# Rotary tables loaded in the opening, memory keys/values through the weights' staging, roundings behind late transfers moved on ScalarE

## The chip, the cores and the metric

One NeuronCore of a Trainium2 chip runs the whole program. Its engines are TensorE (PE in the profile, with PEld for the loading of stationary operands), VectorE (DVE), ScalarE (ACT), GpSimd (POOL) and SyncE (SP), which here only issues DMAs. Time is in device microseconds (us), from runs of the same program on the chip; lower is better. Each engine takes its instructions in the order in which they stand in its program; engines wait for each other through semaphores.

## The reference

An encoder trunk of two layers on 1024 tokens of width 1024, with 256 memory tokens, all in float32. The first layer mixes tokens by windowed attention (16 heads that share 4 key/value heads, rotary positions, a sink per head), the second by a gated linear recurrence (HGRN2, 8 heads, both directions). In both, four further heads attend to the memory tokens. Each layer ends with a gated feed-forward part.

```python
mem_n = rmsnorm(mem, mem_norm_g)
for layer in range(DEPTH):
    u = rmsnorm(h, norm_g[layer, 0])
    mem_kv = mem_n @ w_mem_kv[layer]
    if kind == 0:
        y = mixer_window_attn(u, mem_kv, a_w_in[slot], a_sink[slot], a_w_out[slot], pos)
    elif kind == 1:
        y = mixer_hgrn2(u, mem_kv, b_w_in[slot], lb[0, layer], lb[1, layer], b_norm_g[slot], b_w_out[slot])
    ...
    h = h + rmsnorm(y, norm_g[layer, 1])
    f = conv_ffn(rmsnorm(h, norm_g[layer, 2]), ...)
    h = h + rmsnorm(f, norm_g[layer, 3])

def rope(x, pos):
    ...
    cos = jnp.cos(ang)[None, :, None, :]
    sin = jnp.sin(ang)[None, :, None, :]
    x1, x2 = xf[..., :half], xf[..., half:]
    return jnp.concatenate([x1 * cos - x2 * sin, x2 * cos + x1 * sin], axis=-1)
```

## The kernel before

Every matrix product is made of three products of rounded parts: an operand x is held as h (x rounded to the matmul's format, a copy on ACT) and l (x minus h, a subtraction on DVE), and `mm3` (L82 to L85) adds h·h, h·l and l·h. So every weight and every activation goes through an ACT instruction and a DVE instruction before PE can use it. In the profile L78/L79 are that pair in `wunit`, L88/L89 in `split`, L415/L416 in `read`, L364/L365 in `attend`, L1281/L1282 in `scaled`.

**Weights.** `wunit` (L69) loads one unit of 512 KB through SP's queue into a staging tile `st` (pool `stg`, 4 buffers) and splits it into `wh` and `wl` (pool `ring`, 4 buffers). With `parts=2` the load and the split are made in two halves; only the first unit is.

**Order.** The program is written in one order, and a scheduler orders each engine's instructions by a simulated time with the written order as priority. `tc.issue_after(ins)` queues those instructions of a block that run on the engine of `ins` behind `ins`. Pools are stacked in SBUF; one that is opened after another's release takes its place and waits for its tiles one by one.

**The opening, `start` (L1264).** `memory_kv` (L150) makes keys and values of the memory for both layers: for each layer four units of key weights (`wmk`) and four of value weights (`wmv`), each followed by a `step()` that hands out one piece of side work: the memory's own norm (`memory_rstd`, which also loads the identity), the eight rows `xT` of the transposed input, rounded into `uh`/`ul` (`part`), and the sums of squares of the eight token blocks of x (`square`, ACT, L1293). The results are written to DRAM (`kvd`). Before its first matmul stand the scaled memory columns `mh`/`ml` (8 of them, from `memT`, `scaled`), whose four loads are issued on ACT's queue.

**The first mixer, `window` (L236).** At its head the tables `cos` and `sin` are loaded through SP's queue (L243, L244) into the pool `attn0`, then the window's mask and the sinks. For each of four groups `proj(g)` (L261) projects eight token tiles (24 matmuls each, `pj`, two PSUM banks), rotates them on DVE (L286, L287) with the tables, adds on POOL (L288, L289) and takes v out of PSUM (L291 on ACT, L292 on DVE), which frees the bank. In group 0 `rooted` (L1255) first scales each token tile's part of the tables by its norm. Each add on POOL of group 0 also sends on `second_sums` (L124): a copy of feed-forward weights from DRAM to DRAM on POOL's queue (`w2s`, 1 MB).

`attend(g)` (L313) goes over eight blocks n of 128 tokens: scores, exponentials (L338, ACT), scaling, transposes, product with v, and a copy of the result out of PSUM into `o` (L357, L358). After each second block `o` goes to DRAM (`oT`), or, in group 3, straight into chunks 6 and 7 of `ul` in SBUF (L363), where it is rounded (L364, L365). Between the blocks `cross_unit` (L191) handles the memory heads; its result leaves PSUM by a copy `xo` (L232) from the only bank `po`.

**The first mixer's output, class `Out` (L392).** `begin` (L436) reads chunks 0 to 5 of each token tile back from `oT` (`read`, L411: DMA on SP's queue, then rounding on ACT and DVE) and multiplies them (`kept`) into y0 (copy L448); `finish` adds the rest. `begin` is written after `attend(3)`, but the scheduler spreads it through that time.

**The second mixer, `hgrn` (L925).** For each of eight heads: `proj`, four calls of `direction` (two directions, two halves of the tokens), `output`. `direction` works in the tiles `E` (pool `hg0`, 5 buffers). In the even heads `cross` (L1204) puts two cross units in: with the first, `cross_head` (L184) loads that memory head's keys/values from `kvd` into a tile `kv`, which is one of the five `E` buffers (L1212), splits it into `kvh`/`kvl` (one buffer) and loads the query weights `wxq`.

Of the kernel before, what the change touches and what calls it, by code (L numbers as in the profile page):

```python
# [8 lines left out]
F32 = mybir.dt.float32  # L9
F32R = mybir.dt.float32r  # L10
# [8 lines left out]
P = 128  # L19
# [28 lines left out]
def build(tc, A, out):  # L48
# [20 lines left out]
    def wunit(src, n=1024, pl=None, eng=None, parts=1):  # L69

        tg = ("wh", "wl") if pl is None else ("xwh", "xwl")
        h = (pl or ring).tile([P, 1024], F32R, tag=tg[0], name=tg[0])
        l = (pl or ring).tile([P, 1024], F32R, tag=tg[1], name=tg[1])
        raw = stg.tile([P, 1024], F32, tag="st", name="st")[:, :n]
        for p in range(parts):
            c = slice(p * n // parts, (p + 1) * n // parts)
            nc.sync.dma_start(raw[:, c], src[:, c])
            act.copy(h[:, c], raw[:, c])  # L78
            (eng or dve).tensor_tensor(l[:, c], raw[:, c], h[:, c].bitcast(F32), op=ALU.subtract)  # L79
        return h, l  # L80
# [155 lines left out]
    def window():  # L236
# [4 lines left out]
        cos = ea.tile([P, NT, 32], F32, name="cos")  # L241
        sin = ea.tile([P, NT, 2, 32], F32, name="sin")
        nc.sync.dma_start(cos, A["cos"])  # L243
        nc.sync.dma_start(sin, A["sin"])  # L244
# [67 lines left out]

        def attend(g, qkv):  # L313
            qs, kh, kl, v = qkv
            for b in range(2):
                for nn in range(4):
# [20 lines left out]
                    for j in range(4):  # L337
                        act.activation(sm[:, j, :w], sm[:, j, :w], AF.Exp, bias=st["nm"][:, j:j + 1], scale=0.125,  # L338
                                       accum_out=st["su"][:, j:j + 1])
# [19 lines left out]
                    if nn % 2 == 1 and g == 3:  # L359
                        ts_ = slice((n - 1) * P, (n + 1) * P)  # L360
                        oh, ol = uh[:, 6:8, ts_], ul[:, 6:8, ts_]
                        for hp in range(2):
                            nc.sync.dma_start(ul[hp * 64:(hp + 1) * 64, 6:8, ts_].bitcast(F32), o[:, hp::2, :])  # L363
                        act.copy(oh, ol.bitcast(F32))  # L364
                        dve.tensor_tensor(ol, ol.bitcast(F32), oh.bitcast(F32), op=ALU.subtract)  # L365
                    elif nn % 2 == 1:
                        ts_ = slice((n - 1) * P, (n + 1) * P)
                        for hp in range(2):
                            nc.sync.dma_start(
                                oT[0][2 * g:2 * g + 2, hp * 64:(hp + 1) * 64, ts_].rearrange("a d t -> d a t"),  # L370
                                o[:, hp::2, :])
# [11 lines left out]
        ea.release()  # L383
        attend(3, cur)
        wo0.open()
        y0 = wo0.w1.tile([P, NT, 512], F32, bufs=1, name="y0")
        wo0.begin(psq, ("pj", "pj", "ptq"), [y0[:, t, :] for t in range(NT)])
# [4 lines left out]
    class Out:  # L392
# [18 lines left out]
        def read(self, ks, c0, c1, eng):  # L411
            c = (slice(None), slice(ks[0], ks[-1] + 1), slice(c0, c1))
            raw = ul[c].bitcast(F32)
            eng.dma_start(raw, oT[self.l][ks[0]:ks[-1] + 1, :, c0:c1].rearrange("k p t -> p k t"))
            act.copy(uh[c], raw)  # L415
            dve.tensor_tensor(ul[c], raw, uh[c].bitcast(F32), op=ALU.subtract)  # L416
# [19 lines left out]
        def begin(self, psb, tags, y0):  # L436
            self.psb, self.y0 = psb, y0
            self.banks += [(psb, t, tags.count(t)) for t in tags]
            eng = (nc.sync, act)[self.l]
            for i, t in enumerate(self.order):  # L440
                if i < 2:
                    with tc.high_priority(AHEAD):
                        self.read(self.groups[0], t * P, (t + 1) * P, eng)
                else:
                    self.read(self.groups[0], t * P, (t + 1) * P, eng)
                ps = self.bank()
                self.kept(ps, t, self.groups[0], True, True)
                act.copy(y0[t], ps)  # L448
            self.used = 0
# [475 lines left out]
    def hgrn():  # L925
# [278 lines left out]
        def cross(n):  # L1204
# [3 lines left out]
            for _ in range(n):  # L1208
                xh_, xb_ = units.pop(0)
                if xhead[1] != xh_:  # L1210
                    xhead[1] = xh_
                    raw = early.tile([P, 512], F32, tag="E", bufs=5, name="kv")  # L1212
# [40 lines left out]
    xss = x0.tile([P, NT], F32, name="xss")  # L1253

    def rooted(t, *tables):  # L1255
# [3 lines left out]
        for x in tables:  # L1259
            dve.tensor_scalar_mul(x, x, rs0[:, c])  # L1260
# [3 lines left out]
    def start():  # L1264
# [8 lines left out]
        pool.memset(ones, 1.0)  # L1273
        act.activation(ones[:, 0:1], ones[:, 0:1], AF.Square)
        act.dma_start(gT, A["gT"])
        first = [wunit(A["wmk"][0, 0], parts=2)]
        for k in range(0, KT, 2):
            act.dma_start(mT[:, k:k + 2], A["memT"][:, k:k + 2])

        def scaled(h, l, raw, g):  # L1280
            act.activation(h, raw, AF.Identity, scale=g)  # L1281
            dve.scalar_tensor_tensor(l, raw, g, h.bitcast(F32), op0=ALU.mult, op1=ALU.subtract)  # L1282

        for k in range(KT):
            scaled(mh[:, k], ml[:, k], mT[:, k], gT[:, 0, k:k + 1])
# [9 lines left out]
        def memory_rstd():  # L1295
# [3 lines left out]
            nc.sync.dma_start(ident, A["ident"])  # L1299
            dve.tensor_scalar(mss, mss, 1.0 / D, EPS, op0=ALU.mult, op1=ALU.add)  # L1300
# [124 lines left out]
```

## Time and profile before

| | us |
|---|---|
| runs shown, median (lowest to highest) | 2672.87 (2672.17 to 2677.5) |
| the profiled execution's own time | 2679.56 |
| its span, first to last instruction | 2677.8 |
| mean granted TensorE clock | 0.993 |

The profile is of one execution. A row of a timeline gives the start, the duration, the engine, the line, the operation, what it writes and reads, the number of instructions merged, and in brackets how long the engine was idle before it and what ended that. A row of windows gives a stretch, its length, the busy time and the number of instructions of each engine (PE, PEld, DVE, ACT, POOL), the granted clock of PE, the share of the DMA engines and GB/s. A row of waits reads: who waited, for whom, in total, times, longest. A row of the chain gives start, length and what the end waited for.

### The profile page before, as it was taken

How to read it: one execution, taken by the hardware profiler on the slowest of the kernel's cores; microseconds unless marked ns; L12 is line 12 of the kernel's file. 1: busy time of each engine (PE TensorE's matmuls, PEld its weight loads, DVE VectorE, ACT ScalarE, POOL GpSimd, SP SyncE). 2: the span in 40 equal slices, each digit the busy share in tenths (PEclk: the TensorE clock that was granted, in tenths of full speed). 3: DMA queues.
4: the chain of work that ended last, by engine and by line, in shares of the span. 5: the costliest groups of instructions: out<-in, count | busy, mean ns of one | idle time of the engine just before them, and what ended most of it. 6: DMA issues, size and time to landing. Idle time of an engine off the chain costs nothing.

```text
span 2677.8 us, 39101 instructions
## 1 busy us (share of the span) xinstructions
PE 2612.1 (98%) x14420; PEld 2192.2 (82%) x14420; DVE 1814.1 (68%) x3041; ACT 1379.2 (52%) x2501; POOL 471.8 (18%) x519
## 2 busy tenths in 40 slices
PE   8899999999999999999999999999999999999998
PEld 7788887788888887887887888888788788888887
DVE  5588786578565655478778686886757755656447
ACT  6467676545444444454455554545534444444443
POOL 0331110211111100032223142230211111110013
PEclk9899999999999999999999999999999999999999
DMA  9583123367777757574325252102436778774666
GB/s 359 203 196 71 60 75 103 96 186 184 207 194 201 204 157 241 195 242 150 99 96 163 76 128 62 48 29 90 143 119 176 193 195 210 197 203 160 225 191 235
DMA packets 195728, 425.93 MB, mean 159 GB/s; under 512 B 20048, under 2 KB 56272, under 8 KB 189904
## 3 DMA queue, kind: packets, MB, share of 16 engines
q1 hardware_dynamic: 161552, 324.59, 37.7%
q0 software_dynamic: 24544, 90.19, 16.2%
q10 hardware_dynamic: 9440, 8.66, 1.0%
q8 instruction: 113, 1.85, 0.3%
q14 instruction: 79, 0.65, 0.1%
HBM read 330.04 MB, written 116.39 MB: 167 GB/s over the span
## 4 chain that ended last, share of the span: by engine, by line
PE 77%; DVE 13%; DMA 4%; ACT 3%; issue 2%; POOL 1%; SPq 0%; ACTq 0%; DVEq 0%; POOLq 0%
PE X L521 27%; PE V L521 11%; PE pj L83 5%; PE pj L84 5%; PE pj L85 5%; PE Y L521 5%; PE pb L83 3%; PE pb L85 3%; PE pb L84 3%; DVE E L1077 1%; DVE ER L1112 1%; PE pt L351 1%; PE po L1180 1%; DVE wl L89 1%; DVE wl L79 1%
## 5 line engine op out<-in xcount | busy, mean ns | idle before, releaser
L89 DVE TENSOR_TENSOR wl<-st,wh 128x1024 fp32r<-128x1024 f32 (+1 forms) x238 | 262.6, 1110 | 326.9 <-ACT wh L88 283.3
L88 ACT CAST wh<-st 128x1024 fp32r<-128x1024 f32 (+1 forms) x238 | 222.5, 937 | 295.7 <-PE X L521 194.0
L83 PE MATMUL pj<-uh,wh 128*128 128x512 f32 x512 | 205.4, 402 | 2.2 <-DVE q L1022 1.4
L521 PE MATMUL X<-wl,wh 128*128 128x512 f32 x528 | 205.3, 391 | 0.3 <-DVE wl L89 0.3
L521 PE MATMUL X<-wh,wl 128*128 128x512 f32 x528 | 205.1, 390 | 0.0
L84 PE MATMUL pj<-ul,wh 128*128 128x512 f32 x512 | 203.1, 397 | 0.1
L83 PE MATMUL pj<-wh,uh 128*128 128x384 f32 (+1 forms) x512 | 190.6, 373 | 13.0 <-DVE v L292 9.2
L85 PE MATMUL pj<-uh,wl 128*128 128x512 f32 x512 | 202.7, 396 | 0.0
L521 PE MATMUL X<-wh 128*128 128x512 f32 x528 | 199.5, 391 | 2.2 <-ACT c L894 2.2
L85 PE MATMUL pj<-wh,ul 128*128 128x384 f32 (+1 forms) x512 | 187.5, 367 | 0.0
L84 PE MATMUL pj<-wl,uh 128*128 128x384 f32 (+1 forms) x512 | 187.3, 366 | 0.0
L79 DVE TENSOR_TENSOR wl<-st,wh 128x1024 fp32r<-128x1024 f32 (+2 forms) x94 | 118.5, 1267 | 36.4 <-ACT wh L78 35.7
L521 PE MATMUL V<-uh,wh 128*128 128x512 f32 x344 | 133.8, 389 | 0.0
L521 PE MATMUL V<-ul,wh 128*128 128x512 f32 x344 | 133.8, 389 | 0.0
L521 PE MATMUL V<-uh,wl 128*128 128x512 f32 x344 | 133.8, 389 | 0.0
L78 ACT CAST wh<-st 128x1024 fp32r<-128x1024 f32 (+2 forms) x100 | 99.8, 1006 | 45.3 <-PE pj L84 28.5
L521 PEld LDWEIGHTS X<-wh 128*128 128x128 f32 x528 | 99.5, 188 | 23.5 <-ACT c L894 2.6
L521 PEld LDWEIGHTS X<-wl,wh 128*128 128x128 f32 x528 | 99.6, 189 | 21.3 <-DVE wl L89 0.7
L83 PEld LDWEIGHTS pj<-wh,uh 128*128 128x128 f32 x512 | 97.0, 189 | 24.4 <-issue 9.4
L521 PEld LDWEIGHTS X<-wh,wl 128*128 128x128 f32 x528 | 99.4, 188 | 20.8
L83 PEld LDWEIGHTS pj<-uh,wh 128*128 128x128 f32 x512 | 97.4, 190 | 22.1 <-DVE q L1022 2.2
L85 PEld LDWEIGHTS pj<-uh,wl 128*128 128x128 f32 x512 | 97.2, 190 | 19.7
(388 smaller groups left out, 7163.0 us busy)
## 6 DMA issues: line engine op xcount, KB each, us to landing
st<-hid SPq DMA_DIRECT2D x154, 256.0 KB, 3.0
st<-in_ffw_dram SPq DMA_DIRECT2D x108, 256.0 KB, 3.3
w2s<-in_ffw_dram POOLq DMA_DIRECT2D x24, 1024.0 KB, 7.8
st<-in_ffw_dram SPq DMA_DIRECT2D x46, 512.0 KB, 4.2
hid<-tt SPq DMA_DIRECT2D x88, 256.0 KB, 4.8
st<-w2s SPq DMA_DIRECT2D x88, 256.0 KB, 3.3
sx<-in_ffw_dram SPq DMA_DIRECT2D x84, 256.0 KB, 4.0
sy<-in_ffw_dram SPq DMA_DIRECT2D x42, 512.0 KB, 6.5
```

Of the source, the lines that this page charges most:

```text
L78: act.copy(h[:, c], raw[:, c])
L79: (eng or dve).tensor_tensor(l[:, c], raw[:, c], h[:, c].bitcast(F32), op=ALU.subtract)
L83: pe.matmul(o, ah, bh, start=first, stop=False)
L84: pe.matmul(o, ah, bl, start=False, stop=False)
L85: pe.matmul(o, al, bh, start=False, stop=last)
L88: act.copy(h, src)
L89: dve.tensor_tensor(l, src, h.bitcast(F32), op=ALU.subtract)
L351: pe.transpose(tp[:, j, :], sm[:, j, c * P:(c + 1) * P], ident)
L521: pe.matmul(o, x, y, start=new, stop=e, skip_group_check=not first)
L1077: dve.tensor_tensor_scan(B[:, rev], smask, a_[:, rev], 0.0, op0=ALU.mult, op1=ALU.add)
L1112: dve.tensor_tensor(re_, re_, bc(pl_[:, :, e:e + 1], [P, nb, n]), op=ALU.mult)
L1180: pe.matmul(po[:, c, :], x, y, start=i == 0, stop=i == len(ops) - 1)
```

## The change

Five edits:

1. The tables `cos` and `sin` get a pool of their own, opened before `start`, and are loaded in `memory_rstd` behind the identity. The pool is released after group 3's projection, just below `attn0`.
2. The opening: `gT` and the first two pieces of `memT` are issued on ACT's queue ahead of ACT's first activation, the other two pieces on SP's queue behind the two halves of the first weight unit. That unit is split in quarters (`fourth`), and between the quarters stand pairs of memory columns; `issue_after` fixes this order on ACT.
3. In group 3 of `attend` the rounding of a pair of blocks (`split_moved`) is written behind the next even block's exponentials, and its ACT half is queued behind the last of them; for the last pair it stays where it was.
4. In `begin` the ACT rounding of the reads of token tiles 6 and 7 is queued behind the last exponential of block 1 of group 3 (`marks[3, 1]`).
5. In the second mixer `kv` is a staging tile `st` in place of an `E` tile.

```diff
@@ -66,17 +66,15 @@
-    def wunit(src, n=1024, pl=None, eng=None, parts=1):
+    def wunit(src, n=1024, pl=None, eng=None):
 ...
         raw = stg.tile([P, 1024], F32, tag="st", name="st")[:, :n]
-        for p in range(parts):
-            c = slice(p * n // parts, (p + 1) * n // parts)
-            nc.sync.dma_start(raw[:, c], src[:, c])
-            act.copy(h[:, c], raw[:, c])
-            (eng or dve).tensor_tensor(l[:, c], raw[:, c], h[:, c].bitcast(F32), op=ALU.subtract)
+        nc.sync.dma_start(raw, src)
+        act.copy(h[:, :n], raw)
+        (eng or dve).tensor_tensor(l[:, :n], raw, h[:, :n].bitcast(F32), op=ALU.subtract)
         return h, l
@@ -238,10 +236,6 @@
         psp = tc.alloc_tile_pool(name="aps", bufs=1, space=PSUM, side="right", reuse_waits="tile")
-        cos = ea.tile([P, NT, 32], F32, name="cos")
-        sin = ea.tile([P, NT, 2, 32], F32, name="sin")
-        nc.sync.dma_start(cos, A["cos"])
-        nc.sync.dma_start(sin, A["sin"])
         wmask = ap_.tile([P, 384], F32, bufs=1, name="wmask")
@@ -310,6 +304,14 @@
+        marks, moved = {}, []
+
+        def split_moved():
+            ts_ = moved.pop()
+            oh, ol = uh[:, 6:8, ts_], ul[:, 6:8, ts_]
+            act.copy(oh, ol.bitcast(F32))
+            dve.tensor_tensor(ol, ol.bitcast(F32), oh.bitcast(F32), op=ALU.subtract)
+
         def attend(g, qkv):
@@ -335,8 +337,11 @@
                     for j in range(4):
-                        act.activation(sm[:, j, :w], sm[:, j, :w], AF.Exp, bias=st["nm"][:, j:j + 1], scale=0.125,
-                                       accum_out=st["su"][:, j:j + 1])
+                        marks[g, n] = act.activation(sm[:, j, :w], sm[:, j, :w], AF.Exp, bias=st["nm"][:, j:j + 1],
+                                                     scale=0.125, accum_out=st["su"][:, j:j + 1])
+                    if moved and n % 2 == 0:
+                        with tc.issue_after(marks[g, n].ins):
+                            split_moved()
                     dve.tensor_tensor(st["su"], st["su"], st["es"], op=ALU.add)
@@ -358,11 +363,11 @@
                         ts_ = slice((n - 1) * P, (n + 1) * P)
-                        oh, ol = uh[:, 6:8, ts_], ul[:, 6:8, ts_]
+                        moved.append(ts_)
                         for hp in range(2):
                             nc.sync.dma_start(ul[hp * 64:(hp + 1) * 64, 6:8, ts_].bitcast(F32), o[:, hp::2, :])
-                        act.copy(oh, ol.bitcast(F32))
-                        dve.tensor_tensor(ol, ol.bitcast(F32), oh.bitcast(F32), op=ALU.subtract)
+                        if n == NT - 1:
+                            split_moved()
                     elif nn % 2 == 1:
@@ -381,10 +386,11 @@
         ea.release()
+        tables.release()
         attend(3, cur)
 ...
         y0 = wo0.w1.tile([P, NT, 512], F32, bufs=1, name="y0")
-        wo0.begin(psq, ("pj", "pj", "ptq"), [y0[:, t, :] for t in range(NT)])
+        wo0.begin(psq, ("pj", "pj", "ptq"), [y0[:, t, :] for t in range(NT)], {6: marks[3, 1], 7: marks[3, 1]})
         psp.release()
@@ -408,11 +414,12 @@
-        def read(self, ks, c0, c1, eng):
+        def read(self, ks, c0, c1, eng, behind=None):
             c = (slice(None), slice(ks[0], ks[-1] + 1), slice(c0, c1))
 ...
             eng.dma_start(raw, oT[self.l][ks[0]:ks[-1] + 1, :, c0:c1].rearrange("k p t -> p k t"))
-            act.copy(uh[c], raw)
+            with tc.issue_after(behind.ins) if behind else nullcontext():
+                act.copy(uh[c], raw)
             dve.tensor_tensor(ul[c], raw, uh[c].bitcast(F32), op=ALU.subtract)
@@ -433,7 +440,7 @@
-        def begin(self, psb, tags, y0):
+        def begin(self, psb, tags, y0, behind={}):
             self.psb, self.y0 = psb, y0
@@ -442,7 +449,7 @@
                 else:
-                    self.read(self.groups[0], t * P, (t + 1) * P, eng)
+                    self.read(self.groups[0], t * P, (t + 1) * P, eng, behind.get(t))
                 ps = self.bank()
@@ -1209,7 +1216,7 @@
                     xhead[1] = xh_
-                    raw = early.tile([P, 512], F32, tag="E", bufs=5, name="kv")
+                    raw = stg.tile([P, 1024], F32, tag="st", name="st")[:, :512]
                     xhead[0] = cross_head(1, xh_, wp, raw.rearrange("p (a b) -> p a b", a=2))
@@ -1251,12 +1258,15 @@
     xss = x0.tile([P, NT], F32, name="xss")
-
-    def rooted(t, *tables):
+    tables = tc.alloc_tile_pool(name="tables", bufs=1, reuse_waits="tile")
+    cos = tables.tile([P, NT, 32], F32, name="cos")
+    sin = tables.tile([P, NT, 2, 32], F32, name="sin")
+
+    def rooted(t, *turns):
         c = slice(t, t + 1)
 ...
         pool.tensor_tensor(rs0[:, c], xss[:, c], nhalf[:, c], op=ALU.pow)
-        for x in tables:
+        for x in turns:
             dve.tensor_scalar_mul(x, x, rs0[:, c])
@@ -1271,18 +1281,45 @@
         pool.memset(ones, 1.0)
+        act.dma_start(gT, A["gT"])
+        for k in (0, 2):
+            act.dma_start(mT[:, k:k + 2], A["memT"][:, k:k + 2])
         act.activation(ones[:, 0:1], ones[:, 0:1], AF.Square)
-        act.dma_start(gT, A["gT"])
-        first = [wunit(A["wmk"][0, 0], parts=2)]
-        for k in range(0, KT, 2):
-            act.dma_start(mT[:, k:k + 2], A["memT"][:, k:k + 2])
 ...
         def scaled(h, l, raw, g):
-            act.activation(h, raw, AF.Identity, scale=g)
+            ins = act.activation(h, raw, AF.Identity, scale=g)
             dve.scalar_tensor_tensor(l, raw, g, h.bitcast(F32), op0=ALU.mult, op1=ALU.subtract)
-
-        for k in range(KT):
-            scaled(mh[:, k], ml[:, k], mT[:, k], gT[:, 0, k:k + 1])
+            return ins
+
+        def column(k):
+            return scaled(mh[:, k], ml[:, k], mT[:, k], gT[:, 0, k:k + 1])
+
+        def fourth(p):
+            c = slice(p * 256, (p + 1) * 256)
+            act.copy(wh0[:, c], raw0[:, c])
+            dve.tensor_tensor(wl0[:, c], raw0[:, c], wh0[:, c].bitcast(F32), op=ALU.subtract)
+
+        wh0, wl0 = [ring.tile([P, 1024], F32R, tag=x, name=x) for x in ("wh", "wl")]
+        raw0 = stg.tile([P, 1024], F32, tag="st", name="st")
+        for p in range(2):
+            nc.sync.dma_start(raw0[:, p * 512:(p + 1) * 512], A["wmk"][0, 0, :, p * 512:(p + 1) * 512])
+        for k in (4, 6):
+            nc.sync.dma_start(mT[:, k:k + 2], A["memT"][:, k:k + 2])
+        fourth(0)
+        column(0)
+        with tc.issue_after(column(1).ins):
+            fourth(1)
+            column(2)
+            ahead = column(3)
+        with tc.issue_after(ahead.ins):
+            fourth(2)
+            column(4)
+            ahead = column(5)
+        with tc.issue_after(ahead.ins):
+            fourth(3)
+            column(6)
+            column(7)
+        first = [(wh0, wl0)]
@@ -1297,6 +1334,8 @@
             nc.sync.dma_start(ident, A["ident"])
+            nc.sync.dma_start(cos, A["cos"])
+            nc.sync.dma_start(sin, A["sin"])
             dve.tensor_scalar(mss, mss, 1.0 / D, EPS, op0=ALU.mult, op1=ALU.add)
```

## The prediction

> **What bounds the kernel now.** I read the page first, then who TensorE (PE) waits for, then the chain of waits that ended last, and then the timeline around each DMA in that chain.
>
> ```profile
> span 2677.8 us, 39101 instructions
> PE 2612.1 (98%) x14420; PEld 2192.2 (82%) x14420; DVE 1814.1 (68%) x3041; ACT 1379.2 (52%) x2501; POOL 471.8 (18%) x519
> ...
> PE pj L83 <- DVE v L292: 9.2, 3, 7.5
> PE pb L83 <- ACT mh L1281: 7.8, 1, 7.8
> ...
> PE po L83 <- ACT xo L232: 2.0, 1, 2.0
> ...
> 62.50 6.88 DMA cos<-in_cos_dram
> ...
> 408.20 3.74 DMA ul<-oT
> ...
> 1450.40 7.84 DMA kv<-kvd
> ```
>
> PE is busy 98% of the span, so an edit is worth only what it takes out of PE's idle time, or out of its time at a lower clock. The idle time of the whole span is 2677.8 - 2612.1 = 65.7 us at most. Two waits stand out, 7.5 us (three waits on v come to 9.2) and the first 7.8 us. Three of the chain's transfers are those that the change touches: the rotary tables, a read of oT and the memory keys/values kv.
>
> **Part 1, the tables.** They are issued today behind the last rows of x:
>
> ```profile
> 62.07 0.38 SPq L1292 DMA_DIRECT2D x<-in_x_dram  x1
> 62.50 0.66 SPq L243 DMA_DIRECT2D cos<-in_cos_dram  x1
> ...
> 69.41 0.24 DVE L1260 TENSOR_SCALAR cos<-cos,rs 128x32 f32<-128x32 f32 x1 [7.79 <-DMA cos<-in_cos_dram]
> ...
> 55.46 0.33 PE L83 MATMUL pj<-wh,uh 128*128 128x384 f32 x1
> 71.82 0.66 PE L83 MATMUL pj<-wh,uh 128*128 128x384 f32 x1 [7.53 <-DVE v L292]
> ...
> 64.00:72.00 8.00, 0.47 (x3) 0.21 (x2) 1.89 (x8) 4.29 (x8) 0.93 (x2) 0.69 0.78 286
> 72.00:77.28 5.28, 5.28 (x17) 5.28 (x18) 2.42 (x9) 0.32 (x1) 3.73 (x7) 0.50 0.69 234
> ```
>
> PE starts the first projection at 55.46, finishes two token tiles in the two PSUM banks at 71.82 - 7.53 = 64.29, and stands 7.53 us. After that it runs 5.28 us at clock 0.50 (column PEclk of the windows), which costs half of that, 2.64 us. Loaded with the memory's first steps, the tables land long before 64; both terms go: 7.53 + 2.64 = 10.17 us is the most this can give.
>
> What is late next is ScalarE (ACT), which takes its instructions in order:
>
> ```profile
> 65.58 1.06 ACT L1293 ACTIVATE x<-x 128x1024 f32<-128x1024 f32 x1 [3.91 <-DMA x<-in_x_dram]
> ...
> 69.13 1.06 ACT L1293 ACTIVATE x<-x 128x1024 f32<-128x1024 f32 x1 [1.13 <-DMA x<-in_x_dram]
> ...
> 71.05 0.31 ACT L291 ACTIVATE v<-pj,rs 128x64 fp32r<-128x64 f32 x1 [0.77 <-DVE xss L1257]
> ```
>
> Squares of the last blocks of x (5 and 7 of 0 to 7 are shown) wait for their transfers and end at 69.13 + 1.06 = 70.2. A PSUM bank is free 0.77 us after its v starts (71.05 to 71.82). Three orders are possible. All eight v behind the last square: the first bank is free at 70.2 + 0.8 = 71.0, 0.9 us sooner than today. Only from the second v on behind it: that bank is free at 71.0, and PE, at (64.29 - 55.46)/2 = 4.4 us a tile, asks for it at 68.7: a stall of 2.3. Only from the third on: none, since that one is asked for at 73.1. Without a wait on cos the first v is done 2.4 us (69.41 to 71.82) after the first tile, at 59.9 + 2.4 = 62.3, before block 5 lands at 65.6, so I take the middle order and a rest of 2.3. **Term: -10.2 + 2.3 = -7.9 us**, bounds -10.2 and -0.9.
>
> A rest of 2.3 raises the question of the clock:
>
> ```profile
> 100.00:112.00 12.00, 8.80 (x32) 6.74 (x31) 8.10 (x30) 5.45 (x16) 8.76 (x11) 0.72 0.79 268
> 404.00:418.00 14.00, 11.15 (x55) 8.53 (x56) 9.90 (x26) 8.46 (x21) 0.00 (x0) 1.00 0.46 134
> ```
>
> Of 100 to 112 us 3.2 were idle, in several pieces, and the clock fell to 0.72 on average, so (1 - 0.72)/0.5 x 12 = 6.7 us were run at half speed, 3.4 us lost. Of 404 to 418 2.85 were idle, most in one piece of 2.03, and it stayed at 1.00. A single rest of 2.3 is most like the second, so nothing is added. The Trainium skill ("TensorE: Matmul & The Clock Gate", section on HAM oscillation) says that PE falls to half speed when it idles through a whole window of about 3.4 us. By that rule the term would be -7.9, by the first row -7.9 + 3.4 = -4.5; the first row doesn't agree with it, as its 3.2 us are less than one window, and the second does.
>
> **Part 2, the opening.** First unit of weights in quarters, memT partly on SP's queue, tables (0.39 MB) ahead of the fourth key unit.
>
> ```profile
> 3.74 0.62 ACT L78 CAST wh<-st 128x512 fp32r<-128x512 f32 x1 [1.07 <-DMA st<-in_wmk_dram]
> 6.22 0.62 ACT L78 CAST wh<-st 128x512 fp32r<-128x512 f32 x1 [1.87 <-DMA st<-in_wmk_dram]
> 7.21 0.91 ACT L1281 ACTIVATE mh<-mT,gT 128x256 fp32r<-128x256 f32 x2 [0.37 <-issue]
> ...
> 7.77 0.58 PE L83 MATMUL pb<-mh,wh 128*128 128x256 f32 x1 [7.77 <-ACT mh L1281]
> ...
> 14.00:15.00 1.00, 1.00 (x11) 1.00 (x10) 0.06 (x1) 1.00 (x4) 0.00 (x0) 1.00 1.01 401
> ...
> 17.84 1.22 DVE L79 TENSOR_TENSOR wl<-st,wh 128x1024 fp32r<-128x1024 f32 x1
> ...
> 19.23 0.36 PE L83 MATMUL pb<-mh,wh 128*128 128x256 f32 x1
> ```
>
> Today ACT waits for the second half of the first unit before it rounds the first column of memory. In the new order a quarter and two columns come ahead of that half; PE could start as early as 3.74 + 0.31 + 0.46 = 4.5, 3.3 us sooner, if the first memT has landed by then, and at 6.22 + 0.46 = 6.7, 1.1 sooner, if memT lands only with that half. But the DMA engines are full (share 1.01 at 14 to 15 us), and the fourth unit is split at 17.84 + 1.22 = 19.06 for a matmul at 19.23: 0.17 us of reserve. The 0.39 MB take 0.39 MB / 401 GB/s = 1.0 us of the engines and push that unit back. An earlier start then only meets a wait there. **Term: +0.5 us**; bounds -3.3, and +4.4 (the 1.0 of the tables, and the 3.4 that the clock took at 100 to 112).
>
> **Part 3, roundings moved on ACT.**
>
> ```profile
> 411.96 0.83 ACT L415 CAST uh<-ul 128x768 fp32r<-128x768 f32 x1 [2.55 <-DMA ul<-oT]
> 412.70 0.58 ACT L232 COPY xo<-po 128x512 f32<-128x512 f32 x1
> ...
> 413.33 0.50 PE L83 MATMUL po<-ph,kvh 128*128 128x512 f32 x1 [2.03 <-ACT xo L232]
> ...
> 427.94 0.62 ACT L338 ACTIVATE sm<-sm,nm 128x384 f32<-128x384 f32 x1
> ...
> 448.39 0.59 ACT L448 COPY y<-pb 128x512 f32<-128x512 f32 x1 [0.75 <-PE pb L85]
> ...
> 460.75 0.62 ACT L364 CAST uh<-ul 128x512 fp32r<-128x512 f32 x1 [1.65 <-DMA ul<-o]
> ```
>
> ACT stands 2.55 us on the read of token tile 6; the copy xo queued behind frees the only bank po, and PE waits 2.03. With the two casts behind the exponentials of block 1 xo goes at 411.96 - 2.55 = 409.4, when ACT is free. Tile 6's own matmuls are near its copy y at 448, over 20 us later, so nobody waits for the late cast. The roundings of L364 keep their place: that at 460.75 comes after the exponentials of block 2 already (427.94), so naming these changes nothing there; its 1.65 is ACT's alone. **Term: -2.0 us**; bounds -2.6 (all of ACT's 2.55) and +1.7, if a wait like that at 460.75 comes to stand before PE.
>
> **Part 4, kv through the staging.**
>
> ```profile
> 1458.26 0.62 ACT L88 CAST kvh<-kv 128x512 fp32r<-128x512 f32 x1 [5.77 <-DMA kv<-kvd]
> ...
>   ACT E L1070: 11.7, 4
> ...
> 1443.00:1480.00 37.00, 33.82 (x304) 27.80 (x292) 27.02 (x55) 16.94 (x38) 16.70 (x17) 1.00 0.73 149
> 1609.00:1640.00 31.00, 29.79 (x308) 24.76 (x299) 27.77 (x54) 16.02 (x35) 11.83 (x12) 1.00 0.19 43
> 1771.00:1800.00 29.00, 26.67 (x253) 22.08 (x254) 26.12 (x50) 16.72 (x36) 9.08 (x9) 1.00 0.07 19
> ```
>
> kv takes one of five E buffers, so its load waits for one, and the next direction's E waits until kv is split (11.7 us of ACT in four waits, beside 5.77 on the load). PE covers nearly all of it with projections: its idle time in the three windows is 3.2 + 1.2 + 2.3 = 6.7 us, and other waits are in that. Through the staging, kv is loaded as the weights around it are. It takes a staging buffer from them for one load, and its cast can still stand at ACT's head for a late landing, as at 1458. **Term: -1.5 us**, between -6.7 and +6.0 (all four loads as dear as the first window's 3.2, with 1.2 and 2.3 there already and none in the first head: 3.2 + 2.0 + 0.9).
>
> **Sum:** -7.9 + 0.5 - 2.0 - 1.5 = -10.9 us. The profiled execution took 2679.56 us (span 2677.8 and 1.76 around it) and would take 2668.7. The median of the runs shown, 2672.87, lies 6.7 below it; taken off that, the forecast is **2662.0**.
>
> **Rivals.** (a) *Squares hold v* (15%): all v stay behind the last square; part 1 gives 0.9 of idle time. 2672.87 - 0.9 + 0.5 - 2.0 - 1.5 = 2669. For it: that is today's order. Against: today v has nothing to gain by going earlier, as cos lands last.
> (b) *The copies collide, slower* (10%). POOL's adds of the rotation start the copies w2s:
>
> ```profile
> 71.08 0.86 POOL L288 TENSOR_TENSOR rq<-t,t 128x320 f32<-128x320 f32 x1 [21.84 <-DVE sk L379]
> ...
> 72.16 0.77 POOL L140 DMA_DIRECT2D w2s<-in_ffw_dram  x1
> ```
>
> With the tables early the first add comes near 61.5 instead of 71.08, and the second 4.4 later; each sends a copy of 1 MB (2.6 us at 401 GB/s) into engines still busy with the rows of x. The last square moves from 70.2 to 75.4. If all v are behind it, PE stands until 76.2, 4.4 longer than today: 2672.87 + 4.4 + 0.5 - 2.0 - 1.5 = 2674.3. It decides from where that square ends after 71 with the first v behind it. Against: what speaks against (a), and that the rows of x issued before 61.5 go first.
> (c) *Everything lands* (15%): no rest in part 1, -10.2; opening -1.1; part 3 -2.6; part 4 half its bound, -3.4: -17.3, 2655.6.
> (d) *kv only moves its wait* (10%): a landing later than the order was made for puts a stall like the 5.77 before other work at each of the four loads; part 4 costs its 6.0: -7.9 + 0.5 - 2.0 + 6.0 = -3.4, 2669.5. For it: only one of today's loads landed late, with the engines 0.73 busy. Against: nothing then waits for kv but its own split.
>
> **How the numbers follow.** Forecast 50%, in its own range 2657 to 2666. A change under 0.2% (5.3 us) can't be told from none here. Faster by more than that, below 2667.5: forecast and (c), with a third of (a) and (d), 0.73. Slower, above 2678.2: half of (b), and 0.03 for upper bounds that add up, 0.08. Within: the rest, 0.19. The range for 8 in 10 is 2655 to 2671.
>
> **What would show it.** Right: no PE wait on v above 2.5 us before 80 us and clock 1.00 from 64 to 80; no wait of xo near 411; no E waiting on kvl in the second mixer. Wrong: the last square still ahead of the first v; PE waiting at the fourth key unit for more than 2 us; ACT idle over 5 us on kv; copies w2s landing before the rows of x. The forecast falls if PE's first projection still stands over 5 us.

## The result, and the profile after

| | before | after |
|---|---|---|
| median (lowest to highest), 6 runs each on the same chip | 2675.19 (2672.17 to 2679.22) | 2695.12 (2692.44 to 2701.31) |
| the profiled execution | 2679.56 | 2701.31 |
| its span | 2677.8 | 2699.2 |
| mean granted TensorE clock | 0.993 | 0.991 |

The ratio is 1.0075, 95% interval 1.0065 to 1.0086: the change costs 20 us where 10.9 were forecast as a gain. First the page of the kernel after, its totals, and its list of what PE waited for (total, times, longest):

```profile
span 2699.2 us, 39095 instructions
PE 2617.6 (97%) x14420; PEld 2195.7 (81%) x14420; DVE 1811.0 (67%) x3043; ACT 1378.0 (51%) x2503; POOL 470.7 (17%) x519
```

```profile
PE pj L81 <- DVE v L286: 9.4, 4, 6.3
PE pb L81 <- ACT mh L1290: 7.4, 1, 7.4
PE pj L81 <- DVE q L1029: 6.8, 4, 2.7
PE pt L1197 <- DVE on L1193: 5.8, 2, 3.5
PE pj L81 <- DVE gs L1015: 4.7, 2, 3.9
...
PE pt L1158 <- ACT ot L1205: 3.8, 2, 3.6
...
PE pu L1163 <- ACT kT L1160: 2.8, 1, 2.8
```

The wait on v, which the tables were to remove, is still 6.3 us long; the wait on xo is gone. The waits on q, `on`, gs, ot and kT have grown or are new; all of them belong to the second mixer. Its price can be read from a window that begins and ends at the same two instructions of each kernel, the first projection's wait on s and the last output's wait on `on`. The first row is before, the second after; the columns are the stretch, its length, busy time (instructions) of PE, PEld, DVE, ACT, POOL, then PE's clock, the DMA share, and GB/s.

```profile
1260.84:1930.30 669.46, 657.50 (x5224) 554.81 (x5224) 519.28 (x1014) 354.18 (x765) 171.00 (x183) 1.00 0.32 92
```

```profile
1256.18:1948.78 692.60, 667.19 (x5224) 560.42 (x5224) 515.56 (x1014) 352.01 (x766) 169.96 (x183) 0.99 0.31 89
```

The stretch starts 4.7 us earlier than before and ends 18.5 us later. With the same 5224 matmuls it is 692.60 - 669.46 = 23.1 us longer: 13.4 us of it are PE's idle time (25.4 instead of 12.0), and 9.7 us are busy time, the same matmuls at a lower clock. The next windows of the kernel after show where that clock went:

```profile
1436.00:1448.00 12.00, 8.10 (x29) 6.23 (x28) 10.47 (x24) 5.13 (x18) 5.81 (x8) 0.86 0.38 132
1550.00:1572.00 22.00, 16.55 (x89) 13.04 (x83) 12.40 (x24) 10.01 (x19) 3.24 (x4) 0.92 0.51 127
1610.00:1622.00 12.00, 8.39 (x36) 6.53 (x35) 11.09 (x24) 6.51 (x21) 5.07 (x7) 0.86 0.52 109
1890.00:1905.00 15.00, 11.44 (x102) 9.06 (x101) 10.64 (x18) 10.33 (x18) 2.68 (x2) 0.77 0.45 146
```

Taken as stretches at half speed, these are 3.4, 3.5, 3.4 and 6.9 us (for the first, 12 x 0.14 / 0.5), 17.1 in all, and half of that, 8.6 us, is lost: most of the 9.7.

A part of the loss begins on ScalarE, near the third memory head's load. This is ScalarE's timeline in the kernel after; in brackets stands the idle time before an instruction, and what ended it:

```profile
1550.55 0.62 ACT L1078 ACTIVATE E<-E 128x512 f32<-128x512 f32 x1
1551.20 0.72 ACT L1079 ACTIVATE E<-E,lb 128x512 f32<-128x512 f32 x1
1558.29 0.62 ACT L86 CAST kvh<-st 128x512 fp32r<-128x512 f32 x1 [6.36 <-DMA st<-kvd]
1558.81 0.72 ACT L1081 ACTIVATE s<-s,lno 128x512 f32<-128x512 f32 x1
1559.44 0.56 ACT L1160 COPY kT<-pt 128x512 f32<-128x512 f32 x1
...
1560.42 0.60 ACT L991 ACTIVATE q<-pj 128x512 f32<-128x512 f32 x1
```

and these are PE's two waits just behind it:

```profile
1560.05 1.16 PE L1163 MATMUL pu<-v,kT 128*128 128x128 f32 x8 [2.76 <-ACT kT L1160]
...
1565.27 0.50 PE L81 MATMUL pj<-uh,wh 128*128 128x512 f32 x1 [2.70 <-DVE q L1029]
```

The cast of kv stands between the second logarithm (L1079) and the next exponential (L1081) of a running `direction`, and s, kT, As and q of the recurrence are behind it on ACT. None of them needs kv. ACT stood 6.36 us for it. (That ScalarE takes its queue strictly in order is also what the Trainium skill says, "TensorE: Matmul & The Clock Gate", section on the architectural detail of the array.) The chain of waits within 1540 to 1570 us has the load as its largest piece:

```profile
1547.68 1.99 DVE wl L77
...
1549.69 8.58 DMA st<-kvd
...
1558.29 0.62 ACT kvh L86
...
1565.27 0.50 PE pj L81
```

It also shows why the load is late: it can go out only when a weight's split (wl) gives its staging buffer back. Over the whole kernel ACT stood for kv three times, 13.4 us in all:

```profile
ACT kvh L86 <- DMA st<-kvd: 13.4, 3, 6.4
```

In the second and the fourth head, too, a q stands behind the cast, and PE waited 1.58 us (at 1392.74) and 1.44 us (at 1736.13) for it. PE's waits right behind the three casts are then 2.76 + 2.70 + 1.58 + 1.44 = 8.5 us, with 1.8 us of clock (half of the 3.5 above). That is less than half of the 23.1 us. The three longest waits of this mixer are others:

```profile
1442.54 0.47 PE L81 MATMUL pj<-wh,uh 128*128 128x512 f32 x1 [3.90 <-DVE gs L1015]
...
1616.27 0.30 PE L1197 MATMUL pt<-ident,on 128*128 128x128 f32 x1 [3.49 <-DVE on L1193]
...
1897.76 1.11 PE L1158 MATMUL pt<-ident,ER 128*128 128x128 f32 x4 [3.56 <-ACT ot L1205]
```

No load of kv is in the chains that end at them. The first two go back over a scan of 2.25 us on DVE to a product of the direction (pa) for which ACT had stood 4.83 us; the third goes back over the store of a memory head's result (4.44 us) to a read of oT (5.29 us). These waits come with edit 5 all the same: edit 5 alone, shown below, has 3.90 and 3.49 us in the same places, and 1.49 in the third. What leads from kv's new place to them isn't shown; the build orders all engines anew for each program, and that may be all.

Before, the cast at 1458.26 waited 5.77 us as well; behind it stood the next direction's first exponential and a gs for which PE waited 1.14 us, and PE's idle time in that window was 3.2 us.

In the first mixer the kernel after still holds v behind the squares (timeline of ACT; L1330 is the square, L285 the first half of v):

```profile
66.25 1.06 ACT L1330 ACTIVATE x<-x 128x1024 f32<-128x1024 f32 x1 [1.96 <-DMA x<-in_x_dram]
...
68.44 1.06 ACT L1330 ACTIVATE x<-x 128x1024 f32<-128x1024 f32 x1 [1.04 <-DMA x<-in_x_dram]
...
69.50 0.29 ACT L285 ACTIVATE v<-pj,rs 128x64 fp32r<-128x64 f32 x1
74.61 0.62 ACT L86 CAST kvh<-kv 128x512 fp32r<-128x512 f32 x1 [4.82 <-DMA kv<-kvd]
77.30 0.31 ACT L285 ACTIVATE v<-pj,rs 128x64 fp32r<-128x64 f32 x1 [2.07 <-DVE xss L1267]
```

The first v starts when the last square is done. Ahead of the second stand two transfers: DVE waits for the sinks, and then for ACT's cast of the first mixer's kv, before it scales that token tile's tables (75.87) and the sum that v needs (xss, 77.10). DVE's wait for the sinks, and PE's waits on v:

```profile
74.07 0.17 DVE L384 TENSOR_SCALAR sk<-sk 128x16 f32<-128x16 f32 x1 [3.97 <-DMA sk<-in_a_sink_dram]
```

```profile
70.25 0.66 PE L81 MATMUL pj<-wh,uh 128*128 128x384 f32 x1 [6.29 <-DVE v L286]
...
78.08 0.41 PE L81 MATMUL pj<-wh,uh 128*128 128x384 f32 x1 [1.51 <-DVE v L286]
```

### The profile page after: what moved, and what is told of

Same layout as the page of the kernel before. It is cut to its first block, busy times and chain, and to the rows that moved or that the text cites. A ratio compares the mean times of both kernels' runs of the same rounds, so it can differ in the third digit from the quotient of the medians.

```text
span 2699.2 us, 39095 instructions
## 1 busy us (share of the span) xinstructions
PE 2617.6 (97%) x14420; PEld 2195.7 (81%) x14420; DVE 1811.0 (67%) x3043; ACT 1378.0 (51%) x2503; POOL 470.7 (17%) x519
## 4 chain that ended last, share of the span: by engine, by line
PE 76%; DVE 12%; ACT 4%; DMA 4%; issue 2%; POOL 1%; SPq 0%; ACTq 0%; DVEq 0%; POOLq 0%
PE X L528 26%; PE V L528 11%; PE pj L81 6%; PE pj L82 6%; PE pj L83 5%; PE Y L528 5%; PE pb L81 3%; PE pb L82 3%; PE pb L83 3%; DVE wl L77 1%; DVE E L1084 1%; PE pt L356 1%; PE pu L1163 1%; PE pa L1112 1%; DVE wl L87 1%
## 5 line engine op out<-in xcount | busy, mean ns | idle before, releaser
L87 DVE TENSOR_TENSOR wl<-st,wh 128x1024 fp32r<-128x1024 f32 (+1 forms) x238 | 262.4, 1109 | 326.6 <-ACT wh L86 320.9
L86 ACT CAST wh<-st 128x1024 fp32r<-128x1024 f32 (+1 forms) x238 | 222.4, 937 | 296.4 <-PE X L528 196.5
L77 DVE TENSOR_TENSOR wl<-st,wh 128x1024 fp32r<-128x1024 f32 (+1 forms) x92 | 120.0, 1309 | 25.6 <-ACT wh L76 25.1
L76 ACT CAST wh<-st 128x1024 fp32r<-128x1024 f32 (+1 forms) x98 | 98.6, 1014 | 37.4 <-PE pj L82 20.0
```

Of the source, the lines that this page charges most:

```text
L76: act.copy(h[:, :n], raw)
L77: (eng or dve).tensor_tensor(l[:, :n], raw, h[:, :n].bitcast(F32), op=ALU.subtract)
L86: act.copy(h, src)
L87: dve.tensor_tensor(l, src, h.bitcast(F32), op=ALU.subtract)
```

## The experiments

Edits are counted as in the list of the change: 1 the tables, 2 the opening, 3 and 4 the two kinds of roundings, 5 the memory keys/values (kv). Ratios are to the kernel before, run in turn on the same chip, with 95% intervals; 0.001 is 2.7 us.

**Which edit carries the loss.** *Edit 5 alone* on the kernel before, and *edits 1 to 4 alone*:

```diff
-raw = early.tile([P, 512], F32, tag="E", bufs=5, name="kv")
+raw = stg.tile([P, 1024], F32, tag="st", name="st")[:, :512]
```

> The kernel before with edit 5 alone (kv of the second mixer in a staging tile). If the 20 us come from edit 5, whatever its mechanism: 2692 to 2698 us, and ACT stands about 13 us on the load of kv in three heads. If they come from edits 1 to 4 moving the second mixer's start by 5 us: 2670 to 2677 us.

> The changed kernel with kv back in an E tile (edits 1 to 4 alone). If edit 5 carries the loss: 2668 to 2674 us, since the changed kernel was 4.6 us ahead at the second mixer's start. If edits 1 to 4 carry it: 2690 us or more.

Measured: edit 5 alone 2700.6 us, ratio 1.0102 (1.0084 to 1.0121); edits 1 to 4 without it 2675.35, ratio 1.0001 (0.9992 to 1.0011). One line carries the whole loss, and the other four edits together move nothing that can be measured. ACT stands 12.6 us on the load of kv in three heads with edit 5 alone, as expected. (Beside edit 5 the other four seem to gain: 1.0102 becomes 1.0075 in the whole change; the intervals just meet, and why is open.)

**Late cast, still through the staging.** The split of kv is queued on ACT behind the last instruction of `direction` just ahead of the cross units (the copy kT):

```diff
-        split(kvh, kvl, raw)
+        with tc.issue_after(behind.ins) if behind else nullcontext():
+            split(kvh, kvl, raw)
```

> The changed kernel, kv still in staging and still loaded early, but its split queued on ACT behind the last ACT instruction of the direction before its cross units, some 65 us later. Theory 'early cast' (the cast stands at ACT's head for a landing, in front of the first q of the head): 2668 to 2676 us. Rival 'staging' (a staging buffer is taken from the weights): the buffer is held far longer, so 2695 us or more. Rival 'E order' (with kv out of the five E buffers the directions come in a worse order): about 2690 us.

Measured: 2681.61, ratio 1.0023 (1.0013 to 1.0033). Some 70% of the loss is gone, with kv still in the staging. The time lies in none of the three ranges that were expected: a staging buffer held longer doesn't cost more, but a cast that late isn't free.

**kv in a tile of its own.** Neither staging nor E: the raw kv goes into the tile `on`, free at that time.

> The changed kernel with kv neither in staging nor in E, but in the tile 'on' that is free from one head's output to the next, so that it is loaded before the head's directions and takes nothing from weights or directions. 'Early cast': 2668 to 2680 us, the cast coming after the head's start. 'Staging': 2668 to 2674 us. 'E order': about 2690 us.

Measured: 2674.16, ratio 0.9998 (0.9988 to 1.0007). That E has its fifth buffer back brings nothing in this build, and the rival by which it costs ("E order", about 2690) is out.

**Cast behind the head's first direction** (staging as in the change; `behind` is that direction's kT), and **kv in place**, early and late: loaded straight into kvl, so that no raw tile is needed.

```diff
+        if raw is None:
+            raw = kvl.bitcast(F32)
         nc.sync.dma_start(raw, kvd[l][h])
```

> The changed kernel with kv in staging, its split queued on ACT behind the last ACT instruction of the head's first direction: past the start of the head, but some 30 us sooner than when it stood behind the third direction (2681.6). 'Early cast': 2674 to 2680 us, since any place past the landing is as good. 'Staging' with a price by the time held: also below 2681.6, near 2678. If the split has to come before the head starts at all: 2690 us or more.

> The changed kernel, but kv is loaded straight into kvl and split there, with no staging buffer and no E buffer. It can be loaded and split as early as in the changed kernel, as soon as the cross units before it are done. 'Early cast': 2690 us or more, though no staging is taken, with ACT standing about 13 us on the load. 'Staging': 2674 us.

> As the one before, in place in kvl, with the split queued on ACT behind the direction before its cross units. It differs from the kernel that took 2681.6 us only in that no staging buffer is held. If holding the buffer cost those 6 us: 2672 to 2676 us. If the place of the split cost them: 2680 to 2683 us.

Measured: behind the first direction 2672.74, ratio 0.9982 (0.9972 to 0.9992); in place 2672.26, 0.9979 (0.9967 to 0.9990); in place and late 2678.27, 1.0010 (1.0000 to 1.0019). The first says that staging costs nothing where the cast has time. The second says that my expectation of "early cast" (2690 or more) was too simple: in place, the cast is early too, ACT waits 8.9 us in three heads for it, and nothing is lost. The third lies between its two expectations: the very late place of the cast costs about 8 us against the early one ((1.0010 - 0.9979) x 2675), with no staging buffer held, and whether the buffer adds to that (1.0023 with it) is at the limit of the intervals. ACT's timeline with kv in place shows the difference (third memory head):

```profile
1540.16 0.62 ACT L86 CAST kvh<-kvl 128x512 fp32r<-128x512 f32 x1 [4.10 <-DMA kvl<-kvd]
1540.97 0.69 ACT L1207 ACTIVATE ot<-pt,bng 128x512 f32<-128x512 f32 x1 [0.19 <-DMA oT<-xo]
...
1542.93 0.72 ACT L1083 ACTIVATE s<-s,lno 128x512 f32<-128x512 f32 x1
```

Here the cast stands ahead of ot, not between the logarithms and s, and its 4.10 us lie in the time in which ot waits for its own transfer (the 0.19 us behind it are left of that; before, ot alone waited 4.13 there). The load went out at 1534.98, 1.1 us ahead of ACT's issue of xo's store at 1536.09; in the changed kernel that store is issued at 1545.86 and the load 3.8 us behind it, at 1549.69. Measured from the same point it is 4.9 us earlier in place, as it waits for PE's last use of kvl (a matmul at 1534.56; the profile names the projection matmul beside it) and not for a staging buffer. So two things differ at once, the landing and the place. SyncE's waits around that load, in place and in the changed kernel:

```profile
SPq L187 <- PE pj L83: 6.6, 1, 6.6
```

```profile
SPq L185 <- DVE wl L77: 11.2, 1, 11.2
SPq L75 <- DMA st<-kvd: 7.3, 1, 7.3
```

The second of the lower rows is the query weights' load: it in turn waits for kv to leave the staging.

**The two taken apart.** kv in place (early load), its cast fixed at the place on ACT that it has in the changed kernel:

```diff
+            ln = act.activation(a_, a_, AF.Ln, bias=1.0, scale=lb[:, d, h:h + 1])
+            if hook:
+                hook(ln)
...
+   direction(h, r, d, b, qin[d], S[d], As, prepare if (h, i) == (0, 0) or h % 2 and i == 2 else None)
```

(`prepare`, the hook, loads the next memory head's kv into kvl and splits it under `issue_after(ln)`.)

> Edits 1 to 4, kv loaded straight into kvl, and its cast fixed on ScalarE at the very place that it has in the changed kernel: behind the second logarithm of a direction of the odd head, ahead of that direction's s, kT, As and q. Only the load differs: it needs no staging buffer. Theory 'late landing': the load goes out at the end of the key/value units, as in the run with kv in place (1534.98, landed 1540.14), lands before ScalarE reaches the cast (1558 - 6.4 = 1552 in the changed kernel, near 1543 in that run's time), ScalarE does not stand, and the time is that of the run in place, 2672 +- 4. Theory 'place': a cast there, ahead of s, kT and q, costs by standing there; 2690 or more with the load early as well.

Measured: 2679.5, ratio 1.0014 (1.0005 to 1.0023), between the two theories. ACT doesn't stand at the cast any more:

```profile
1548.41 0.73 ACT L1084 ACTIVATE E<-E,lb 128x512 f32<-128x512 f32 x1
1549.05 0.60 ACT L86 CAST kvh<-kvl 128x512 fp32r<-128x512 f32 x1
1549.55 0.72 ACT L1088 ACTIVATE s<-s,lno 128x512 f32<-128x512 f32 x1
```

By the ratios, this kernel gains (1.0075 - 1.0014) x 2675 = 16 us on the changed one by its early load, and loses (1.0014 - 0.9979) x 2675 = 9 us against kv in place and early, by the place of the cast. Neither difference is that one thing alone: each build orders all engines anew, and here the load of the query weights is written apart from kv's. Of the changed kernel's long waits not only those behind the casts are gone, but also the 3.49 us on `on` and the 3.56 on ot, whose chains hold no kv. What is left of the loss shows near the second memory head: a 3.89 us wait on gs, which the changed kernel has too (the 3.90 us above), and in the clock (the same window, in this kernel and with kv in place and early):

```profile
1436.00:1448.00 12.00, 10.49 (x53) 8.18 (x55) 6.02 (x17) 2.34 (x6) 5.40 (x7) 0.72 0.39 99
```

```profile
1436.00:1448.00 12.00, 11.69 (x56) 9.82 (x57) 10.90 (x23) 6.89 (x15) 4.77 (x6) 1.00 0.84 175
```

Why that order leads to a late gs isn't settled.

**The squares.** Edits 1 to 4, and the squares of x blocks 5 to 7 queued behind v of token tiles 0 to 2:

```diff
-                     + [tuple(lambda t=t: square(A["x"], t, xss) for t in (5, 6, 7))])
...
+                    if g == 0 and t < 3:
+                        s = 5 + t
+                        xr = stg.tile([P, 1024], F32, tag="st", name="st")
+                        nc.sync.dma_start(xr, A["x"][s * P:(s + 1) * P, :])
+                        with tc.issue_after(out_of.ins):
+                            act.activation(xr, xr, AF.Square, accum_out=xss[:, s:s + 1])
```

> Edits 1 to 4 alone (2675.4 us), with the squares of token blocks 5, 6 and 7 queued on ACT behind the v of tiles 0, 1 and 2, their rows of x in staging tiles. If PE's wait at 64 us is held by these squares and not by the tables any more: the wait of 5.5 us falls under 2.3, and 2667 to 2671 us. If something else holds v (DVE behind the sinks' load, POOL): the wait stays above 4 us and 2674 to 2677 us.

> The kernel before with one edit: squares of x blocks 5 to 7 queued behind v of tiles 0 to 2, the tables late as before. If both, the late tables and the squares, hold the first projection (each hides the other): v alone is free but q and k of the first group wait for cos (landed 71), PE's wait of 7.5 us near 64 stays within 2 us, and the time is 2672 to 2677, no difference to before. If the squares alone were the limit and the tables worth nothing: 7 less, 2668.

Measured: with edits 1 to 4 2668.83, ratio 0.9972 (0.9960 to 0.9984); alone, with the tables late as before, 2677.1, ratio 0.9997 (0.9988 to 1.0006). Tables without squares (edits 1 to 4) 1.0001, squares without tables 0.9997, both 0.9972: by the whole time each hid the other. By the trace not wholly: alone, the squares shortened PE's wait on v from 7.53 to 4.31 us, more than the 2 us that I had allowed for, and the whole time doesn't show it. Nor is it ACT's order alone that the two edits change: with the rows of x in the staging, SP's queue comes sooner to the sinks and kv (issued at 61.92 and 62.44 instead of 69.99 and 70.68), for which the second v had to wait. With both, the window 60 to 80 us has 19.05 us of PE at clock 1.00, where the changed kernel has 12.20 at 0.83 (the two rows in that order), and PE's longest wait on v there is 0.95 us.

```profile
60.00:80.00 20.00, 19.05 (x111) 18.62 (x110) 9.52 (x39) 6.60 (x16) 10.11 (x17) 1.00 0.94 318
```

```profile
60.00:80.00 20.00, 12.20 (x59) 11.63 (x59) 4.96 (x18) 5.94 (x12) 4.72 (x8) 0.83 0.68 226
```

**The roundings alone**, edits 3 and 4 on the kernel before:

> The kernel before with edits 3 and 4 alone (the two casts of the read of token tiles 6 and 7, and those of the last group's pairs, behind later exponentials). By the prediction: -2.0 (bounds -2.6 and +1.7), so 2673 where before is 2675, with the wait of 2.03 us on xo near 411 gone. By the rival 'the wait moves': the wait near 411 goes, new ones of up to 3 us stand near 371 and 479, and the time is that of before within 1 us.

Measured: 2673.89, ratio 0.9993 (0.9984 to 1.0001): -1.9 us, with an interval that just holds no change at all. The wait on xo is gone here, and no new one of over 1.2 us came in 360 to 500 us; the changed kernel's 1.8 us on o and 2.8 on pl, which edits 1 to 4 have too (1.8 and 2.5), come only with the other edits.

**What beats both.** Edits 1 to 4, the squares, and kv in place:

> Edits 1 to 4, the squares of x blocks 5 to 7 behind v of tiles 0 to 2, and kv loaded straight into kvl, without staging and without E. If the two gains lie in different stages and add up: the squares gave 2668.8 where edits 1 to 4 alone gave 2675.4 (-6.5), in place gave 2672.3 where they gave 2675.4 (-3.1), so 2675.4 - 6.5 - 3.1 = 2665.8, below both kernels. If in place gains nothing once the first mixer is earlier: 2669. Span of the profiled run 2658 to 2668.

Measured: 2666.53, ratio 0.9961 (0.9947 to 0.9975), 10.4 us below before. The two gains, 0.0029 and 0.0022 below edits 1 to 4, would add up to 0.9950; the interval holds that, but also the 0.9972 of the squares without kv in place, so that they add up is not shown.

## Why the prediction was wrong

**Part 4, the step that failed.** I bounded kv's move by +6.0, from PE's idle time around the loads of *before*, with the reason that nothing then waits for kv but its own split. That bound carries a price from one place to another. In the new place the cast had s, kT, As and q behind it on an engine that takes its instructions in order, and the load had to wait for a staging buffer. Alone, the edit cost 25.7 us more by the median (edit 5 alone 2700.6 against 2674.87), four times my upper bound. The changed kernel's trace puts 8.5 us of PE's waits and 1.8 us of clock right behind the casts; the rest stands in the waits on gs, `on` and ot, which come with edit 5 by a way that stays open. So a price by what stands behind the cast would have been nearer, and still too low. The rival "kv only moves its wait" had the mechanism, the late landing in front of other work, and I gave it a chance of 10% and that same bound as its price. I also wrote that the cast "can still stand at ACT's head for a late landing", and took -1.5 all the same. The row that should have widened the bound was in the prediction: 5.77 us of ACT for a late landing, which at four loads is 23; that this comes near the 25.7 is luck, as ACT stood for kv in three heads and 12.6 us.

The gain that I counted, by E's fifth buffer with its 11.7 us of ACT's waits before, did not come with the buffer alone (kv in a free tile, 0.9998); that fits ACT's waits lying under PE's projections, as I had noted. In place, 0.9979 against 1.0001 is a gain of 5.9 us, more than the term of -1.5 and inside its bound of -6.7. An early landing isn't its source for certain, as the cast behind the head's first direction gains as much (0.9982) with kv in the staging.

**Part 1, a second step that failed.** Without part 4 the forecast was -9.4 us, and edits 1 to 4 measured 1.0001. I took the middle one of three orders, the first v ahead of block 5's square, for -7.9. The build kept all squares ahead of the first v: rival (a), which I gave 15%. Three of the signs named for a wrong forecast came: the last square ahead of the first v, PE's stand of over 5 us in the first projection, and ACT idle for over 5 us on kv. With the squares moved the gain is (1.0001 - 0.9972) x 2675 = 7.8 us, give or take 4. That this equals my -7.9 is luck: there three v go ahead of the last square, the order for which the prediction has no rest and -10.2, and the interval doesn't tell the two apart. What I had not priced was the second v, held until 77.30 behind the loads of the sinks and of kv. PE's two waits, 6.29 + 1.51 = 7.80 us, and the 1.9 us that the half clock took of its 3.75 busy us in the row below, make 9.7 us against the 7.53 + 2.64 = 10.2 of before:

```profile
67.00:74.00 7.00, 3.75 (x12) 3.78 (x13) 0.28 (x1) 1.75 (x5) 0.00 (x0) 0.52 0.66 217
```

Of rival (b), the first copy w2s did go out earlier, at 65.25, beside the last block of x. Its square was done at 69.5 all the same, 0.7 ahead of before, not at 75.4 as that rival had it. And a single rest of 2.3 us is not free of the clock, as I took it to be from one row: the kernel before has a wait of 2.25 us that cost it (last section).

**Part 2, inside its bounds, but the other way.** PE's first matmul came at 7.43 us instead of 7.77 and that of the fourth unit at 18.95 instead of 19.23: -0.3 by the trace against +0.5 forecast. The wait that I expected at the fourth unit, for the tables ahead of it, didn't come: after its first matmul PE waits for nothing until the first v. That the start itself gained only 0.3 us is the first memT's landing: ACT stands 2.79 us for it, until 6.87.

**Part 3, right as far as it can be seen.** -2.0 forecast, -1.9 measured alone, which can't be told from none; the wait on xo went as forecast. Inside the whole change the waits on o and pl took its place, which shows no more than that the order changed.

**The base.** I took the profiled 2679.56 to lie above the usual time and worked from the median 2672.87 of three runs. In the experiments the kernel before gave medians of 2674.87 to 2676.65 over 25 and 27 runs, between 2671.27 and 2683.39; so the median of three was some 3 us low. The ratios are free of that.

## What to carry to other kernels

Before a load is moved to another buffer, look at what stands behind its first reader on that reader's engine: on an engine that takes its instructions in order a cast that waits for a transfer holds back everything behind it, and its price is that of the work behind, not that of the load. Then expect the new order to move waits elsewhere too, as more than half of the loss here was not behind the cast. Where two causes end one wait within a microsecond or two of each other, removing either alone gave nothing in the whole time here, so look for the second cause in the trace before the first is changed, and change both. A buffer that needs no turn in a ring (here the low half's own tile) can make a load early without holding anything else.

## What the runs showed of the hardware

The clock fell to half not only behind single waits of 3.5 to 3.9 us. In the changed kernel it also fell behind the second of the two waits of 2.76 and 2.70 us shown above (1550 to 1572 us: 0.92 on average, 3.5 us at half speed), but not behind the first. And it fell behind two shorter single waits, the first in the kernel before, the second in the run with the cast behind the head's first direction:

```profile
1932.55 1.01 PE L1190 MATMUL pt<-ident,on 128*128 128x128 f32 x4 [2.25 <-DVE on L1186]
```

```profile
1553.80 0.50 PE L81 MATMUL pj<-uh,wh 128*128 128x512 f32 x1 [2.28 <-DVE q L1030]
```

The clock was 0.53 from 1934 to 1936 us behind the first and 0.50 from 1556 to 1558 us behind the second. The 2.03 us of the kernel before near 411, and a wait of 2.17 us with the squares alone (at 1461.06, clock 1.00 from 1461 to 1469 us), left it at 1.00. So the length of a wait alone didn't settle it: 2.25 us brought the clock down in one place, and 2.76 us didn't in another. The Trainium skill ("TensorE: Matmul & The Clock Gate", section on HAM oscillation) asks for an idle stretch of a whole window of about 3.4 us; the single long waits agree with that, those of 2.25, 2.28 and 2.70 us don't. The page's next section, on cycling through PSUM banks, names short idle pieces between groups of matmuls as a second cause, without a length; 100 to 112 us of the kernel before, 0.72 with no single wait of over 1.1 us, bears that one out. So a stall of two to three microseconds is to be priced with the chance of a fall, which in the changed kernel cost half of 3.5 us, 1.8 us, on top of the 5.46 us that PE stood.

The same load of kv, 256 KB, took from 2.6 to 8.6 us to land. Its DMA issues (count, size, time to landing) in the kernel before from 1779 to 1784 us, where it is alone, and in the changed kernel from 1540 to 1563 us, beside two copies of 1 MB:

```profile
kv<-kvd SPq DMA_DIRECT2D x1, 256.0 KB, 2.6
```

```profile
w2s<-w2s POOLq DMA_DIRECT2D x2, 1024.0 KB, 8.8
...
st<-kvd SPq DMA_DIRECT2D x1, 256.0 KB, 8.6
```
